# A two-block layer stack on one core: gelu copied out of PSUM in the recurrence, weight splits at phase ends on VectorE, and last products placed behind transposes

## The chip, the core and the metric

The kernel runs on one core of a Trainium2 chip. The metric is the device time of one execution in microseconds. Before the change three runs gave a median of 1570.56 us (1567.63 to 1571.66). One further execution was profiled; everything read from the trace is of that one.

## The reference

The input is one sequence of 256 tokens of width 1024 with a 256-token context. It passes two layers of a first block (latent attention, multi-scale pooling, gated linear attention, merged), then two layers of a second block: an attention layer and a recurrent layer, each followed by a gated feed-forward network. The change touches the second block and the last product of the first. What it computes there, cut to what matters:

```
def rmsnorm_2(x, g):                       # over the 1024 columns
    y = xf * lax.rsqrt(jnp.mean(xf * xf, axis=-1, keepdims=True) + RMS_EPS)
    return y * g

def recurrent_mixer(h, w_in, conv_w, conv_b, w_a, b_a, w_i, b_i, lam, w_out):
    gate, xr = jnp.split(h @ w_in, 2, axis=-1)
    gate = jax.nn.gelu(gate, approximate=True)
    xc = <causal convolution of width 4 on xr, per channel> + conv_b
    r = sigmoid(einsum('bsni,nij->bsnj', xg, w_a) + b_a)     # xg: xc in 4 blocks of 256
    i = sigmoid(einsum('bsni,nij->bsnj', xg, w_i) + b_i)
    log_a = -LRU_C * r * softplus(-lam);  a = exp(log_a)
    u = sqrt(-expm1(2 * log_a)) * (i * xc)
    hs = <scan over tokens: hs[t] = a[t] * hs[t-1] + u[t]>
    return (hs * gate) @ w_out

for layer in range(DEPTH):                 # second block: attention, then recurrence
    x = x + rmsnorm_2(mixer(rmsnorm_2(x, norm_mix_pre)), norm_mix_post)
    x = x + rmsnorm_2(swiglu(rmsnorm_2(x, norm_ffn_pre)), norm_ffn_post)
```

## The kernel before, in words

All matrix products of fp32 data are made of three products of reduced type. An operand is split into a rounded high part and the low rest: for a weight chunk (128 x 1024, 512 KB, tile `wr`) ScalarE copies the high part (`wh`, line 377) and VectorE or GpSimd subtracts it from the raw chunk (`wl`, line 379); for an activation ScalarE does the high part (lines 385, 388) and VectorE the low one (386, 389). A product then takes `high*high`, `low*high` and `high*low` on TensorE (lines 395 to 397), so 24 matmuls for one output tile with eight blocks of 128 in the contraction. There are three buffers for raw chunks and three for split ones, with five more "held" ones at the phase ends, three PSUM tiles `mm` for products and three `at` for transposes, scores and gates.

The engine of a low-part split is chosen by a counter: with `lopool[0] = n` each n-th split goes to GpSimd. `load`, which fetches the weights of a whole phase end, sets n to 6; the recurrence sets it to 3; otherwise it is 0 in the second block, which means VectorE alone.

A scheduler orders the instructions of each engine beforehand, by the order in which the kernel names them, by priorities (`tc.high_priority`) and by its own simulation; on the chip each engine works its queue strictly in that order.

A phase end works like this (`out_proj` for the three mixers, the end of `ffn` for the two feed-forward parts). The tokens stand in two tiles of 128. The output product of tile 0 is made, evicted with a square sum and a gain (`out_evac`, 429 and 579), its norm is taken (GpSimd, 419), it is added to the residual stream `xr` (`residual`, 574), normed for the next phase into `xs` (`prenorm`, 429, 553, 419, 557), transposed on TensorE (560) and split into `xnah` and `xnal` (385, 386). Meanwhile TensorE makes the products of tile 1. In `out_proj` a tile has four products of 24 matmuls; in `ffn` the last chunks of weights are held so that tile 1's share of them can be made after tile 0's.

The recurrence (`recurrent_core`) has these pieces. The gate's first four channel blocks of 128 are made with tokens as rows, passed through gelu and transposed back (`flip`) into `gl`. `conv(i)`, i = 0 to 7, makes a product and applies the four taps, three of them on VectorE straight from PSUM (1414). `gates(n)` makes the two gate products for blocks 2n and 2n+1 (1422) and forms a decay `av`, the inside of the square root `mv` (GpSimd squares `av`, 1434) and `iv`. `states(i0, i1)` takes one square root over four blocks on ScalarE (1441), multiplies on GpSimd (1443) and scans on VectorE (1444). The square root needs another function table in ScalarE than the tanh and exp around it. `gelu(i)` for blocks 4 to 7 makes a product, takes gelu with two multiply-adds that read the product in PSUM (1450, 1452), multiplies with the states (1461) and splits the result into rows of `y` (388, 389), which the output product consumes. In the text the gate blocks 4 to 7 are called halves 4 to 7, after the name the changed code gives them.

Of the kernel before, what the change touches and what calls it, by code (L numbers as in the profile page):

```python
# [9 lines left out]
F32 = mybir.dt.float32  # L10
# [3 lines left out]
OP = mybir.AluOpType  # L14
# [259 lines left out]
def trunk_and_stack(ctx, tc, xin, w, vec, rows, cst, msk, tabs, toep, out):  # L274
# [270 lines left out]
    def prenorm(xn, t, g):  # L545

        xt = xr[:, t, :]
        b = xs_tile(edge)
        ss = sm(2)
        for c in range(2):  # L550
            sq(b[:, c * 512:c * 512 + 512], xt[:, c * 512:c * 512 + 512], ss[:, c:c + 1])
        s1 = sm(1)
        V.tensor_scalar(s1, ss[:, 0:1], ss[:, 1:2], EPS, op0=OP.add, op1=OP.add)
        y = rsqrt(s1, 1)
        for k4 in range(2):
            sl = slice(k4 * 512, k4 * 512 + 512)
            V.scalar_tensor_tensor(b[:, sl], xt[:, sl], y, g[:, sl], op0=OP.mult, op1=OP.mult)
            p = atps()
            for k in range(4):
                T.transpose(p[:, k * P:(k + 1) * P], b[:, (4 * k4 + k) * P:(4 * k4 + k + 1) * P], ident)  # L560
            split(xn, (ALL, slice(4 * k4, 4 * k4 + 4), slice(t * P, t * P + P)), p.rearrange("p (k t) -> p k t", k=4))

# [27 lines left out]
    def load(keys):  # L590

        was = lopool[0]
        lopool[0] = 6
        r = [HW(k) if 2 <= i < 2 + NHOLD else W(k) for i, k in enumerate(keys)]
        lopool[0] = was
        return r

    def out_proj(keyf, a, tiles, ops, after):

        chs = load([keyf(cb, hf) for cb in range(4) for hf in range(2)])  # L600
        for i, (tk, xt, gb) in enumerate(tiles):
            ssp = sm(4)
            for cb in range(4):
                out_evac(as2(chs[2 * cb:2 * cb + 2], a, slice(tk, tk + P)), 256, ops[i], cb * 256, ssp[:, cb:cb + 1], gb)
            with tc.high_priority(offset=600):
                residual(xt, ops[i], ssp, 4)
                after(i)
# [793 lines left out]
    def recurrent_core(xn, y, rp):  # L1401
# [14 lines left out]
        def gates(n):  # L1416
# [8 lines left out]
            for m in range(2):  # L1425
                i = 2 * n + m
                p = gate(ra, m)
                t = rp.tile([P, 256], F32, tag="t", name=nm("rt"), bufs=6)
# [4 lines left out]
                t2 = rp.tile([P, 256], F32, tag="t", name=nm("rt"), bufs=6)  # L1433
# [12 lines left out]
        def gelu2(p):  # L1446

            t = rp.tile([P, 256], F32, tag="t", name=nm("rt"), bufs=6)
# [6 lines left out]
        def gelu(i):  # L1455

            if i < 2 * NR:
                t = gl[:, i, :]
            else:
                t = gelu2(ws(W(("rg", i)), xn, 0, 256))  # L1460
            V.tensor_tensor(t, t, mv[:, i, :], op=OP.mult)
            split(y, (ALL, i), t, 0.25)

        gl = rp.tile([P, 2 * NR, 256], F32, name="gl")
# [9 lines left out]
        for t in range(2):  # L1474
            for i in range(NR):
                late.append((i, t, gelu2(as2(chs[2 * i:2 * i + 2], xn, slice(t * P, t * P + P)))))
# [12 lines left out]
        states(4, 8)  # L1489
        for i in range(8):  # L1490
            gelu(i)
        lopool[0] = 0

    def ffn(l, xn, name):
        with ExitStack() as st:
# [39 lines left out]
            for c in range(2):  # L1535
# [10 lines left out]
                for t in range(2):  # L1546
                    if t == 1:
                        held = held[NHOLD:] + held[:NHOLD]
                        for j, (k2, ch) in enumerate(held):
                            part(pd[1], 1, k2, ch, j == R - 1)  # L1550
                    out_evac(pd[t], 512, ops[t], c * 512, ssp[t][:, c:c + 1], g)
                    if c == 1:
                        with tc.high_priority(offset=600):
                            residual(xr[:, t, :], ops[t], ssp[t], 2)
                            after(t)
# [35 lines left out]
```

## Time and profile before

| what | us |
|---|---|
| median of three runs | 1570.56 |
| the profiled execution | 1570.03 |
| its span in the trace | 1568.3 |
| TensorE busy | 1492.4 |
| VectorE busy | 949.9 |
| ScalarE busy | 756.1 |
| GpSimd busy | 360.9 |

The span runs from the first to the last instruction in the trace; 1.7 us of the profiled execution lie around it. In the trace PE is TensorE, DVE is VectorE, ACT is ScalarE, POOL is GpSimd and SP the engine that issues the transfers. Times in the text such as "at 1334.65" are us from the start of the span. The places in the trace: first block until about 907, its output product until 935, attention 935 to 1043, its output product until 1074, feed-forward until 1263, recurrence 1263 to 1339, its output product until 1365, second feed-forward until the end. A row's `[idle <- releaser]` is how long the engine stood still before the row and what ended that.

### The profile page before, as it was taken

What the parts mean: (1) busy time and instruction counts of PE and PEld (TensorE: products, weight loads), DVE (VectorE), ACT (ScalarE), POOL (GpSimd) and SP (SyncE); (2) the same over time, 40 slices, a digit from 0 to 9 for tenths busy, and PEclk for the clock granted to TensorE, in tenths of its full rate; (3) what the DMA queues carried; (4) which work ended last, traced back from release to release, by engine and by line L of the source; (5) the groups of instructions that cost most, each with busy time, mean ns of one, the idle gap of its engine ahead of it and who ended that gap; (6) DMA issues with size and microseconds to landing.
All of it is one profiled execution on the core that took longest, in us unless ns stands there. A gap on an engine that the chain in (4) does not pass through costs nothing.

```text
span 1568.3 us, 25530 instructions
## 1 busy us (share of the span) xinstructions
PE 1492.4 (95%) x10206; PEld 1284.0 (82%) x10206; DVE 949.9 (61%) x1479; ACT 756.1 (48%) x1267; POOL 360.9 (23%) x276
## 2 busy tenths in 40 slices
PE   6999999999999999998989989989999997899998
PEld 3766668787877789777889989869999887799986
DVE  5555435856445576667694764767665577656654
ACT  4444344453323365755644454554444457534443
POOL 1213125735400002336582020311000034100000
PEclk9999999999999999999999999999999999899999
DMA  8323322222334465224337664425556654435564
GB/s 340 121 103 125 121 90 81 66 76 68 108 110 163 144 189 168 95 74 137 104 133 254 196 217 145 132 85 169 165 186 187 217 187 148 140 130 179 185 187 135
DMA packets 65638, 229.79 MB, mean 147 GB/s; under 512 B 7280, under 2 KB 7920, under 8 KB 65392
## 3 DMA queue, kind: packets, MB, share of 16 engines
q1 hardware_dynamic: 65520, 228.16, 44.9%
q8 instruction: 80, 1.31, 0.3%
q14 instruction: 38, 0.31, 0.1%
HBM read 227.09 MB, written 1.05 MB: 145 GB/s over the span
## 4 chain that ended last, share of the span: by engine, by line
PE 77%; DVE 7%; POOL 4%; issue 4%; DMA 4%; ACT 4%; SPq 0%; POOLq 0%; DVEq 0%; ACTq 0%
PE mm L395 21%; PE mm L397 21%; PE mm L396 21%; DMA wr<-in_w_dram 3%; PE at L735 2%; DVE wl L379 2%; PE aux L768 2%; ACT wh L377 1%; PE at L755 1%; POOL wl L379 1%; POOL E L915 1%; POOL qp L895 1%; PE mm L466 1%; PE at L859 1%; PE aux L466 1%
## 5 line engine op out<-in xcount | busy, mean ns | idle before, releaser
L377 ACT ACTIVATE wh<-wr 128x1024 fp32r<-128x1024 f32 x352 | 370.8, 1055 | 424.9 <-PE mm L396 133.5
L379 DVE TENSOR_TENSOR wl<-wr,wh 128x1024 fp32r<-128x1024 f32 x288 | 363.9, 1265 | 287.2 <-ACT wh L377 285.9
L395 PE MATMUL mm<-xnah,wh 128*128 128x256 f32 (+1 forms) x1192 | 367.9, 309 | 11.2 <-DVE rt L1452 10.3
L397 PE MATMUL mm<-xnah,wl 128*128 128x256 f32 (+1 forms) x1192 | 361.9, 304 | 3.0 <-DVE wl L379 2.1
L396 PE MATMUL mm<-xnal,wh 128*128 128x256 f32 (+1 forms) x1192 | 362.0, 304 | 0.2 <-DVE xnal L386 0.2
L395 PEld LDWEIGHTS mm<-xnah,wh 128*128 128x128 f32 x1192 | 226.6, 190 | 27.8 <-DVE rt L1452 10.6
L379 POOL TENSOR_TENSOR wl<-wr,wh 128x1024 fp32r<-128x1024 f32 (+1 forms) x64 | 158.3, 2473 | 353.3 <-ACT wh L377 268.8
L397 PEld LDWEIGHTS mm<-xnah,wl 128*128 128x128 f32 x1192 | 226.6, 190 | 14.9 <-DVE wl L379 2.7
L396 PEld LDWEIGHTS mm<-xnal,wh 128*128 128x128 f32 x1192 | 226.8, 190 | 10.1 <-issue 1.4
L419 POOL TENSOR_TENSOR sm<-sm,minus_half 128x1 f32<-128x1 f32 (+3 forms) x34 | 25.5, 751 | 628.7 <-DVE sm L567 356.3
L395 PE MATMUL mm<-xnbh,wh 128*128 128x512 f32 (+1 forms) x392 | 138.2, 353 | 0.0
L397 PE MATMUL mm<-xnbh,wl 128*128 128x512 f32 (+1 forms) x392 | 136.9, 350 | 0.0
L396 PE MATMUL mm<-xnbl,wh 128*128 128x512 f32 (+1 forms) x392 | 136.7, 349 | 0.0
L395 PE MATMUL mm<-wh,xnah 128*128 128x256 f32 x288 | 84.3, 294 | 8.5 <-ACT xnah L385 6.3
L395 PEld LDWEIGHTS mm<-xnbh,wh 128*128 128x128 f32 x392 | 75.6, 193 | 11.8 <-issue 2.5
L397 PEld LDWEIGHTS mm<-xnbh,wl 128*128 128x128 f32 x392 | 75.6, 193 | 11.2 <-issue 2.4
L396 PEld LDWEIGHTS mm<-xnbl,wh 128*128 128x128 f32 x392 | 75.7, 193 | 11.0 <-issue 2.1
L396 PE MATMUL mm<-wl,xnah 128*128 128x256 f32 x288 | 83.3, 291 | 1.1 <-POOL wl L379 1.1
L397 PE MATMUL mm<-wh,xnal 128*128 128x256 f32 x288 | 82.6, 290 | 0.7 <-DVE xnal L386 0.7
L396 PE MATMUL mm<-wl,hh 128*128 128x512 f32 x176 | 68.8, 391 | 0.0
L397 PE MATMUL mm<-wh,hl 128*128 128x512 f32 x176 | 68.8, 391 | 0.0
L395 PE MATMUL mm<-yh,wh 128*128 128x512 f32 (+1 forms) x192 | 65.6, 342 | 0.9 <-ACT scr L1030 0.9
(365 smaller groups left out, 2895.5 us busy)
## 6 DMA issues: line engine op xcount, KB each, us to landing
wr<-in_w_dram SPq DMA_DIRECT2D x398, 512.0 KB, 3.6
wr<-in_w_dram SPq DMA_DIRECT2D x18, 256.0 KB, 2.7
row<-in_rows_dram SPq DMA_DIRECT2D x8, 512.0 KB, 5.4
xt<-in_xin_dram SPq DMA_DIRECT2D x4, 512.0 KB, 5.8
scr<-in_rows_dram SPq DMA_DIRECT2D x8, 256.0 KB, 4.8
xr<-in_xin_dram SPq DMA_DIRECT2D x2, 512.0 KB, 4.7
xc<-in_xin_dram SPq DMA_DIRECT2D x2, 512.0 KB, 4.7
toep<-in_toep_dram SPq DMA_DIRECT2D x1, 1024.0 KB, 7.0
```

What stands on the lines that cost most here:

```text
L377: S.activation(ch.h, r, AF.Copy)
L379: eng.tensor_tensor(ch.l, r, ch.h.bitcast(F32), op=OP.subtract)
L395: T.matmul(dst, lh, rh, start=first and i == 0, stop=False)
L396: T.matmul(dst, lh, rl, start=False, stop=False)
L397: T.matmul(dst, ll, rh, start=False, stop=last and i == n - 1)
L419: G.tensor_tensor(y, m, minus_half[:, :n], op=OP.pow)
L466: T.matmul(p[32 * j:32 * j + 32, c0:c0 + 256], sc[:, k * 32:k * 32 + 32], r[:, j, :], start=half == 0, stop=half == 1, tile_position=(0, 3 ...
L735: T.matmul(pa[:, :n], qxs[pr, j][:, c0 + qt * P:c0 + qt * P + P], kxs[pr, j][:, :n], start=True, stop=True)
L755: T.transpose(pa[:, k * 256 + qt * P:k * 256 + qt * P + P], r[qt][:, (2 * k2 + k) * P:(2 * k2 + k + 1) * P], ident)
L768: T.matmul(py[64 * j:64 * j + 64, c0:c0 + 256], v[:, k, h * 64:h * 64 + 64], pTs[j][k // 2][:, k % 2, :], start=k == 0, stop=k == nk - 1, ...
L859: T.matmul(pa[c * s:c * s + s, t * 2 * s:(t + 1) * 2 * s], k_[:, i:i + s], q_[:, :, j:j + s], start=True, stop=True, tile_position=(0, c * s))
L895: (V, G)[j].tensor_tensor(b[r, j, :], gq[r], e[r], op=OP.mult)
```

## The change

- `load` no longer sets `lopool`, and the recurrence no longer sets it to 3: all low-part splits of the second block and of the output product ahead of it go to VectorE. Thirteen GpSimd splits become VectorE splits.
- `gelu2` first copies the product out of PSUM to SBUF (`h`, a ScalarE copy), and the square and both multiply-adds read the copy.
- `gl` holds all eight blocks. The recurrence names its pieces in another order: `conv` 0 to 3, `gates(0)`, `conv` 4 and 5, `gates(1)`, `conv(6)`, the first square root, `conv(7)`, four output blocks, and then the gate halves 4 to 7 between `gates(2)`, `gates(3)` and the second square root. The pool `t` has four buffers in place of six.
- At the phase ends the transposes of tile 0 are returned, and tile 1's last product (in `out_proj` the fourth, 24 matmuls; in `ffn` the last held chunk, six matmuls) is tied behind them on TensorE. At the last phase end there are no transposes and nothing is tied.

```
-        was = lopool[0]
-        lopool[0] = 6
-        r = [HW(k) if 2 <= i < 2 + NHOLD else W(k) for i, k in enumerate(keys)]
-        lopool[0] = was
-        return r
+        return [HW(k) if 2 <= i < 2 + NHOLD else W(k) for i, k in enumerate(keys)]
+
+    def behind(tr):
+        return tc.issue_after(tr.ins) if tr is not None else nullcontext()
...
             for cb in range(4):
-                out_evac(as2(chs[2 * cb:2 * cb + 2], a, slice(tk, tk + P)), 256, ops[i], cb * 256, ssp[:, cb:cb + 1], gb)
+                with behind(tr if cb == 3 else None):
+                    d = as2(chs[2 * cb:2 * cb + 2], a, slice(tk, tk + P))
+                out_evac(d, 256, ops[i], cb * 256, ssp[:, cb:cb + 1], gb)
...
-        def gelu2(p):
-            t = rp.tile([P, 256], F32, tag="t", name=nm("rt"), bufs=6)
-            S.activation(t, p, AF.Square, scale=float(np.sqrt(0.044715)))
-            V.scalar_tensor_tensor(t, t, 1.0, p, op0=OP.add, op1=OP.mult)
+        def gelu2(p, h):
+            S.activation(h, p, AF.Copy)
+            t = rp.tile([P, 256], F32, tag="t", name=nm("rt"), bufs=4)
+            S.activation(t, h, AF.Square, scale=float(np.sqrt(0.044715)))
+            V.scalar_tensor_tensor(t, t, 1.0, h, op0=OP.add, op1=OP.mult)
             S.activation(t, t, AF.Tanh, scale=float(np.sqrt(2 / np.pi)))
-            V.scalar_tensor_tensor(t, t, 1.0, p, op0=OP.add, op1=OP.mult)
-            return t
...
+            V.scalar_tensor_tensor(h, t, 1.0, h, op0=OP.add, op1=OP.mult)
+
+        def out(i):
+            t = gl[:, i, :]
             V.tensor_tensor(t, t, mv[:, i, :], op=OP.mult)
             split(y, (ALL, i), t, 0.25)
...
-        lopool[0] = 3
-        for n in range(4):
-            conv(2 * n)
+        def gate_half(i):
+            gelu2(ws(W(("rg", i)), xn, 0, 256), gl[:, i, :])
+
+        for i in range(4):
+            conv(i)
             if late:
                 flip(*late.pop(0))
-            conv(2 * n + 1)
-            if n:
-                gates(n - 1)
+        gates(0)
+        conv(4)
+        conv(5)
+        gates(1)
+        conv(6)
+        states(0, 4)
+        conv(7)
+        for i in range(4):
+            out(i)
+        gate_half(4)
+        gates(2)
+        gate_half(5)
         gates(3)
-        states(0, 4)
+        gate_half(6)
         states(4, 8)
-        for i in range(8):
-            gelu(i)
-        lopool[0] = 0
+        gate_half(7)
+        for i in range(4, 8):
+            out(i)
...
                         for j, (k2, ch) in enumerate(held):
-                            part(pd[1], 1, k2, ch, j == R - 1)
+                            with behind(tr if c == 1 and j == R - 1 else None):
+                                part(pd[1], 1, k2, ch, j == R - 1)
```

How this moves instructions is seen in the order of each engine. First TensorE at the recurrence's output product, before: `mm_13427` is the fourth and last product of tile 1, `at_13327` and `at_13335` the transposes of tile 0, `mm_13540` the first product of the feed-forward part.

```order
L395 MATMUL mm_13427<-wh_13194,xnbh_12358 128x256
L396 MATMUL mm_13427<-wl_13195,xnbh_12358 128x256
L397 MATMUL mm_13427<-wh_13194,xnbl_12359 128x256
L560 MATMUL at_13327<-ct,xs_13318 128x128 x4
L560 MATMUL at_13335<-ct,xs_13318 128x128 x4
L395 MATMUL mm_13540<-wh_13494,xnah_13144 128x256
```

And the same place now, where `mm_13411` is the third product of tile 1, `mm_13439` the fourth (24 matmuls, three shown) and `mm_13552` the first of the feed-forward part.

```order
L395 MATMUL mm_13411<-wh_13194,xnbh_12358 128x256
L396 MATMUL mm_13411<-wl_13195,xnbh_12358 128x256
L397 MATMUL mm_13411<-wh_13194,xnbl_12359 128x256
L560 MATMUL at_13339<-ct,xs_13330 128x128 x4
L560 MATMUL at_13347<-ct,xs_13330 128x128 x4
L395 MATMUL mm_13439<-wh_13200,xnbh_12358 128x256
L396 MATMUL mm_13439<-wl_13201,xnbh_12358 128x256
L397 MATMUL mm_13439<-wh_13200,xnbl_12359 128x256
```

The transposes have moved ahead of the fourth product. The output products of the first block are reordered in the same way, the end of the first feed-forward part by six matmuls; at attention's output product the transposes stood ahead of the fourth product already, and TensorE's order is unchanged there.

ScalarE at the recurrence's output product, before: `wh_13494` to `wh_13524` are the first six weight chunks of the feed-forward part, `scr` the evictions of tile 1's products, `xnah` the high part of tile 0's transposes.

```order
L429 ACTIVATE scr_13396,sm_13342<-mm_13371 128x256
L377 ACTIVATE wh_13512<-wr_13510 128x1024
L429 ACTIVATE scr_13424,sm_13342<-mm_13399 128x256
L377 ACTIVATE wh_13518<-wr_13516 128x1024
L377 ACTIVATE wh_13524<-wr_13522 128x1024
L429 ACTIVATE scr_13452,sm_13342<-mm_13427 128x256
L385 ACTIVATE xnah_13144<-at_13327 128x4x128
```

And now (the six chunks are `wh_13506` to `wh_13536`):

```order
L429 ACTIVATE scr_13408,sm_13354<-mm_13383 128x256
L377 ACTIVATE wh_13524<-wr_13522 128x1024
L429 ACTIVATE scr_13436,sm_13354<-mm_13411 128x256
L377 ACTIVATE wh_13530<-wr_13528 128x1024
L385 ACTIVATE xnah_13156<-at_13339 128x4x128
L385 ACTIVATE xnah_13156<-at_13347 128x4x128
L377 ACTIVATE wh_13536<-wr_13534 128x1024
L429 ACTIVATE scr_13464,sm_13354<-mm_13439 128x256
```

The high part of the transposes stands behind the fifth chunk in place of the sixth.

VectorE in the middle of the recurrence, before, around the last taps of `conv(7)` (`mm_12851`): the scans are `mv<-av,iv`, the output blocks `gl<-gl,mv`.

```order
L1414 SCALAR_TENSOR_TENSOR xconv<-mm_12851,vt,xconv 128x253
L1444 SCALAR_TENSOR_TENSOR mv_12366<-av,iv 128x256
L1430 TENSOR_SCALAR rt_12887<-rt_12887,nsp 128x256
L1444 SCALAR_TENSOR_TENSOR mv_12366<-av,iv 128x256
L1438 SCALAR_TENSOR_TENSOR iv<-iv,xconv 128x256
L1414 SCALAR_TENSOR_TENSOR xconv<-mm_12851,vt,xconv 128x254
L1444 SCALAR_TENSOR_TENSOR mv_12366<-av,iv 128x256
L1461 TENSOR_TENSOR gl<-gl,mv_12366 128x256
L1444 SCALAR_TENSOR_TENSOR mv_12366<-av,iv 128x256
L1461 TENSOR_TENSOR gl<-gl,mv_12366 128x256
L1414 SCALAR_TENSOR_TENSOR xconv<-mm_12851,vt,xconv 128x255
```

And now (`conv(7)` is `mm_12868`, `wl_13104` the split for half 7, `gl` also holds the copies of the halves):

```order
L1448 SCALAR_TENSOR_TENSOR mv_12366<-av,iv 128x256 x2
L1462 TENSOR_TENSOR gl<-gl,mv_12366 128x256
L379 TENSOR_TENSOR wl_13104<-wr_13101,wh_13103 128x1024
L1418 SCALAR_TENSOR_TENSOR xconv<-mm_12868,vt,xconv 128x254
L389 SCALAR_TENSOR_TENSOR xnbl_12359<-gl,xnbh_12358 128x256
L1455 SCALAR_TENSOR_TENSOR rt_12941<-rt_12941,gl 128x256
L1434 TENSOR_SCALAR rt_12953<-rt_12953,nsp 128x256
L1442 SCALAR_TENSOR_TENSOR iv<-iv,xconv 128x256
L1418 SCALAR_TENSOR_TENSOR xconv<-mm_12868,vt,xconv 128x255
```

Here repeated rows between them are left out. The last tap of `conv(7)` now stands behind all four scans and output blocks, two of their low parts and the split for half 7. Further down, six of the eight low-part splits for the output product stand ahead of the last `mv` of `gates(3)`, where it was three on VectorE before.

## Rows read from the trace of the kernel before

**Rows 1.** The page, busy time and share of each engine.
```profile
PE 1492.4 (95%) x10206; PEld 1284.0 (82%) x10206; DVE 949.9 (61%) x1479; ACT 756.1 (48%) x1267; POOL 360.9 (23%) x276
```

**Rows 2.** PE's timeline: start us, us, operation, count, idle before and its releaser.
```profile
915.35 0.38 PE L396 MATMUL mm<-wl,moh 128*128 128x256 f32 x1 [1.81 <-POOL wl L379]
933.63 0.39 PE L395 MATMUL mm<-wh,xnah 128*128 128x256 f32 x1 [1.12 <-ACT xnah L385]
...
1048.19 0.38 PE L396 MATMUL mm<-wl,xnbh 128*128 128x256 f32 x1 [1.28 <-DVE wl L379]
...
1071.18 0.38 PE L395 MATMUL mm<-wh,xnbh 128*128 128x256 f32 x1 [0.88 <-DVE op L579]
1263.49 0.39 PE L395 MATMUL mm<-wh,xnah 128*128 128x256 f32 x1 [0.82 <-ACT xnah L385]
1264.89 0.38 PE L397 MATMUL mm<-wh,xnal 128*128 128x256 f32 x1 [0.65 <-DVE xnal L386]
...
1334.65 0.58 PE L395 MATMUL mm<-xnah,wh 128*128 128x256 f32 x1 [10.35 <-DVE rt L1452]
...
1369.78 0.58 PE L395 MATMUL mm<-wh,xnah 128*128 128x256 f32 x1 [3.79 <-ACT xnah L385]
```

**Rows 3.** Stretches: length, busy (x count) by engine, granted PE clock, DMA, GB/s.
```profile
935.00:940.00 5.00, 4.91 (x28) 4.70 (x28) 4.58 (x7) 2.59 (x6) 2.70 (x2) 0.66 0.76 275
...
1320.00:1350.00 30.00, 18.23 (x129) 17.30 (x128) 20.49 (x39) 18.60 (x34) 8.94 (x8) 0.83 0.52 158
1335.00:1340.00 5.00, 5.00 (x30) 5.00 (x30) 4.88 (x8) 2.60 (x5) 0.27 (x1) 0.65 0.51 137
...
1370.00:1375.00 5.00, 5.00 (x24) 4.95 (x25) 5.00 (x7) 2.83 (x5) 2.99 (x2) 0.50 0.64 212
...
1380.00:1385.00 5.00, 5.00 (x45) 5.00 (x44) 1.62 (x3) 1.36 (x3) 0.00 (x0) 1.00 0.13 51
```

**Rows 4.** GpSimd's timeline, at splits and in the recurrence.
```profile
912.95 2.35 POOL L379 TENSOR_TENSOR wl<-wr,wh 128x1024 fp32r<-128x1024 f32 x1 [66.69 <-DMA wr<-in_w_dram]
...
1254.71 2.90 POOL L379 TENSOR_TENSOR wl<-wr,wh 128x1024 fp32r<-128x1024 f32 x1 [0.15 <-ACT wh L377]
...
1291.48 2.37 POOL L379 TENSOR_TENSOR wl<-wr,wh 128x1024 fp32r<-128x1024 f32 x1 [6.57 <-ACT wh L377]
...
1318.95 3.16 POOL L1434 TENSOR_TENSOR rt<-av 128x256 f32<-128x256 f32 x1 [3.57 <-ACT av L1431]
```

**Rows 5.** VectorE's operations of 1255 to 1350 by form: count, busy us, mean ns.
```profile
L379 DVE TENSOR_TENSOR wl<-wr,wh 128x1024 fp32r<-128x1024 f32 x17 | 21.0, 1241 | 8.5 <-ACT wh L377 8.5
L1444 DVE TENSOR_TENSOR_SCAN mv<-av,iv 128x256 f32<-128x256 f32 x8 | 5.5, 698 | 0.0
...
L1461 DVE TENSOR_TENSOR rt<-rt,mv 128x256 f32<-128x256 f32 x4 | 1.6, 405 | 0.0
```

**Rows 6.** VectorE's timeline.
```profile
1045.47 2.67 DVE L379 TENSOR_TENSOR wl<-wr,wh 128x1024 fp32r<-128x1024 f32 x1 [0.67 <-ACT wh L377]
...
1254.60 3.57 DVE L574 SCALAR_TENSOR_TENSOR xr<-op,sm,xr 128x512 f32<-128x512 f32 x2
...
1266.29 1.42 DVE L574 SCALAR_TENSOR_TENSOR xr<-op,sm,xr 128x512 f32<-128x512 f32 x2 [0.86 <-POOL sm L419]
...
1291.89 1.00 DVE L1414 SCALAR_TENSOR_TENSOR xconv<-mm,vt,xconv 128x253 f32<-128x253 f32 x2 [0.64 <-ACT xconv L1411]
...
1305.82 0.41 DVE L1435 SCALAR_TENSOR_TENSOR mv<-rt,rt 128x256 f32<-128x256 f32 x1
...
1317.09 0.47 DVE L1414 SCALAR_TENSOR_TENSOR xconv<-mm,vt,xconv 128x255 f32<-128x255 f32 x1
```

**Rows 7.** ScalarE's timeline.
```profile
1331.36 1.06 ACT L1441 ACTIVATE mv<-mv 128x1024 f32<-128x1024 f32 x1
...
1340.26 0.42 ACT L388 ACTIVATE xnbh<-rt 128x256 fp32r<-128x256 f32 x1 [2.66 <-DVE rt L1461]
...
1353.64 0.38 ACT L429 ACTIVATE scr<-mm 128x256 f32<-128x256 f32 x1 [3.03 <-PE mm L397]
...
1367.83 1.06 ACT L377 ACTIVATE wh<-wr 128x1024 fp32r<-128x1024 f32 x1 [3.00 <-DMA wr<-in_w_dram]
```

**Rows 8.** The page, transfers by form: count, KB each, median us to landing.
```profile
wr<-in_w_dram SPq DMA_DIRECT2D x398, 512.0 KB, 3.6
```

More of the change, by code (lines that the diff above doesn't have):

```diff
@@ L1 @@
-from contextlib import ExitStack
+from contextlib import ExitStack, nullcontext
 import numpy as np
@@ L1432, in gates @@
                 S.activation(t, t, AF.Tanh, scale=-1.0)
-                t2 = rp.tile([P, 256], F32, tag="t", name=nm("rt"), bufs=6)
+                t2 = rp.tile([P, 256], F32, tag="t", name=nm("rt"), bufs=4)
                 G.tensor_tensor(t2, av[:, i, :], av[:, i, :], op=OP.mult)
@@ L1444, in states @@
                 V.tensor_tensor_scan(mv[:, i, :], av[:, i, :], iv[:, i, :], 0.0, op0=OP.mult, op1=OP.add)
-        def gelu2(p):
-            t = rp.tile([P, 256], F32, tag="t", name=nm("rt"), bufs=6)
-            S.activation(t, p, AF.Square, scale=float(np.sqrt(0.044715)))
-            V.scalar_tensor_tensor(t, t, 1.0, p, op0=OP.add, op1=OP.mult)
-            S.activation(t, t, AF.Tanh, scale=float(np.sqrt(2 / np.pi)))
-            V.scalar_tensor_tensor(t, t, 1.0, p, op0=OP.add, op1=OP.mult)
-            return t
[L1455 to L1460, printed above, removed]
+        def gelu2(p, h):
+            S.activation(h, p, AF.Copy)
+            t = rp.tile([P, 256], F32, tag="t", name=nm("rt"), bufs=4)
+            S.activation(t, h, AF.Square, scale=float(np.sqrt(0.044715)))
+            V.scalar_tensor_tensor(t, t, 1.0, h, op0=OP.add, op1=OP.mult)
+            S.activation(t, t, AF.Tanh, scale=float(np.sqrt(2 / np.pi)))
+            V.scalar_tensor_tensor(h, t, 1.0, h, op0=OP.add, op1=OP.mult)
+        def out(i):
+            t = gl[:, i, :]
             V.tensor_tensor(t, t, mv[:, i, :], op=OP.mult)
             split(y, (ALL, i), t, 0.25)
-        gl = rp.tile([P, 2 * NR, 256], F32, name="gl")
+        gl = rp.tile([P, 8, 256], F32, name="gl")
         chs = load([("rgt", i, hf) for i in range(NR) for hf in range(2)])
@@ L1475, in recurrent_core @@
             for i in range(NR):
[L1476 removed]
+                h = rp.tile([P, 256], F32, tag="t", name=nm("rt"), bufs=4)
+                gelu2(as2(chs[2 * i:2 * i + 2], xn, slice(t * P, t * P + P)), h)
+                late.append((i, t, h))
                 if len(late) > 1:
                     flip(*late.pop(0))
[L1479 to L1481 removed]
+        def gate_half(i):
+            gelu2(ws(W(("rg", i)), xn, 0, 256), gl[:, i, :])
+        for i in range(4):
+            conv(i)
             if late:
                 flip(*late.pop(0))
[L1484 to L1486 removed]
+        gates(0)
[10 more added lines that the diff above has]
+        gate_half(5)
         gates(3)
[L1488 removed]
+        gate_half(6)
         states(4, 8)
[L1490 to L1492 removed]
+        gate_half(7)
+        for i in range(4, 8):
+            out(i)
     def ffn(l, xn, name):
@@ L1554, in ffn @@
                             residual(xr[:, t, :], ops[t], ssp[t], 2)
-                            after(t)
+                            tr = after(t)
         return nxt
```

6 lines of the change are left out of this document (4 added, 2 removed).

## Prediction

> **What bounds the kernel now.** I read the page's engines first: TensorE is busy 1492.4 us of 1568.3 [rows 1], so it bounds the kernel. A faster operation on another engine is worth nothing except where TensorE waits for it. Next came TensorE's timeline, for its waits at the places that the change touches: eight rows, of which the one at 1334.65 (10.35 us) and the one at 1369.78 (3.79 us) are over 2 us [rows 2]. Third, the stretches behind those waits. A 5 us stretch at full speed holds 45 matmuls; behind the 3.79 us wait one holds 24 at a granted clock of 0.50, which is the 1.2 GHz level of the two (1.2 and 2.4), and behind the 10.35 us wait 30 at 0.65 [rows 3]. So a long wait costs twice: once as idle time, once as slow matmuls. Last came the timelines of the engines that end these waits: GpSimd's splits [rows 4], VectorE by form and by time [rows 5, 6], ScalarE [rows 7] and the transfers [rows 8]. I sum against the profiled execution, 1570.0 us, 0.5 below the median of the runs.
>
> **GpSimd's splits go to VectorE.** A split takes 2.35 to 2.90 us on GpSimd [rows 4] and 1.24 on VectorE [rows 5]. At 915.35 TensorE waited 1.81 us for a GpSimd split; on VectorE it is ready 2.35 - 1.24 = 1.1 us sooner: **-1.1**. At 1048.19 it waited 1.28 us for a VectorE split that took 2.67 us [rows 6], more than twice the normal, while GpSimd split another chunk. Without that neighbour it takes 1.24, 1.4 less, but VectorE now does both, and I count **-1.1** (bounds 0 and -1.3).
>
> The other side of this edit is VectorE's load: 13 x 1.24 = 16 us more. Outside the recurrence VectorE is idle 39% of the span [rows 1], and the splits fall where it waits for ScalarE's high part (8.5 us of idle time in front of 17 splits [rows 5]). Where it is not covered it shows in the recurrence, below.
>
> The residual additions show the same contention: two of them took 3.57 us beside a GpSimd split that ran from 1254.71, and 1.42 us later, beside none [rows 4, 6]. The Trainium skill, page "SBUF — State Buffer", section "Who interferes with whom", has it that a VectorE instruction with two SBUF inputs contends with a GpSimd instruction that reads SBUF, and one with at most one SBUF input does not. Our trace agrees: two taps that take the product from PSUM ran 1.00 us, undelayed, beside a split from 1291.48 [rows 4, 6]. The rule speaks against one edit, since gelu's multiply-adds now read two SBUF operands. If half of the eight were stretched by the residual pair's factor, 3.57 / 1.42 = 2.5, that would be 4 x 0.41 x 1.5 = 2.5 us, and the sum by this rule 12.8 in place of the 15.3 below. I do not count it.
>
> **Phase ends.** (a) First block's output product. Now 24 matmuls (24 x 0.11 = 2.7 us, from 45 in 5 us) stand between tile 0's transposes and the next phase. They cover the 1.12 us wait for `xnah` and most of the slow stretch 935 to 940, which has 28 matmuls in place of 45, so (45 - 28) x 0.11 = 1.9 us. Against that, TensorE reaches the transposes 2.7 us sooner and meets `xs` before it is ready: I put a new wait of 1.3 us there, and 0.3 for less cover later. **-1.4** (bounds 0, -3.0).
> (b) Attention. TensorE's order is unchanged. The 0.88 us wait for an eviction goes, since VectorE's residual is no longer stretched: **-0.9** (bounds 0, -1.2).
> (c) First feed-forward part. The waits are 0.82 + 0.65 = 1.5 us [rows 2]. Six matmuls now lie behind the transposes (0.7 us), and the residual pair is 3.57 - 1.42 = 2.1 us shorter: **-1.3** (bounds 0, -1.5).
> (d) Recurrence's output product. The fourth product of tile 0 is evicted at 1353.64 [rows 7], and the feed-forward part starts 16.1 us later at 1369.78, at half clock. ScalarE stands 3.00 us there for a chunk [rows 7], and the transposes' high part is queued behind that chunk, the sixth. In the new order it is behind the fifth. By counts TensorE passes three products (72 x 0.11 = 8 us), the transposes (about 1), then the fourth (2.7): some 12 us after the eviction, when `xnah` and `xnal` are about ready. The idle time of 3.79 goes, and with it the slow clock: (45 - 24) x 0.11 = 2.3 in 1370 to 1375 and about 0.4 beyond. **-6.5** (bounds -3.8, if the clock still falls, and -6.9). This is the surest and largest term. If the sixth chunk were still ahead, the 3.00 would remain.
>
> **Recurrence.** The 10.35 us wait at 1334.65 is one for a gelu multiply-add (line 1452) that frees a PSUM tile; it is late because tanh stood behind the second square root (1331.36) and its table load. The copy frees that tile at once, so this wait in this form goes. In all 129 matmuls stand in 1320 to 1350, where 270 would fit: 141 x 0.11 = 15.7 us are lost there [rows 3]. The question is what is late next, and I think it is VectorE. Its queue from 1306.2 (end of the `mv` at 1305.82 [rows 6]) to the last tap of `conv(7)` now holds three splits (3 x 1.24), six taps (6 x 0.47), four scans (4 x 0.70), four output blocks (4 x 0.40), and two low parts and three small operations (5 x 0.40; no row, taken as line 1461's): 3.7 + 2.8 + 2.8 + 1.6 + 2.0 = 12.9 us, and an estimated 1 us in which it waits for the first square root. So the tap ends at 1320.1; before it ended at 1317.6, and GpSimd's square of the next `av` followed at 1318.95 [rows 4], which shows `gates(3)` right behind that tap. TensorE waits 2.5 us here.
> From there the last `mv` comes 2.5 us later or more, since six splits stand ahead of it on VectorE where three stood (3.7 us more, most of it in idle time). The second square root's end goes from 1332.4 to about 1336.3: 2.5 from the tap, and 1.4 because the weight copies ahead of it on ScalarE wait for chunks that land 3.6 us after their issue [rows 8]. The first row of `y` (1340.26 before, 7.8 after the square root) now comes 4.6 after it, because two splits (2.5 us) and two multiply-adds (0.8) which stood between are done earlier: 1340.9. TensorE, free of gelu, is through with everything else near 1332, and stands some 9 us. Resuming at half clock costs it 1.2 as I guess from the 15 matmuls missing in 1335 to 1340 (15 x 0.11 = 1.7). New loss 2.5 + 9.0 + 1.2 = 12.7 against 15.7: **-3.0**. The bounds are far apart. At best only the tap's 2.5 and a short wait of some 3 remain: -10. At worst the square root stands behind two more landings (2 x 3.6): +4.2. I take -3.0, since the chain to the square root is read from rows and moves by little.
> The eight copies out of PSUM (8 x 0.4 = 3 us, as an eviction in [rows 7]) lie in ScalarE's idle time, half of its span [rows 1]; without that cover they'd delay the square root by under 2. That the halves of the square root are apart changes nothing: the number of table loads is the same. Four buffers of `t` in place of six suffice for four gate halves. Cost 0.
>
> **Sum:** 1.1 + 1.1 + 1.4 + 0.9 + 1.3 + 6.5 + 3.0 = 15.3; 1570.0 - 15.3 = 1554.7, so 1555.
>
> **Rivals.**
> 1. The recurrence gives nothing or gives back up to 3 us: the `y` rows are as late as ever because the square root is, and VectorE's splits delay it further. For it: VectorE's queue there is nearly full (20.49 of 30 us in 1320 to 1350 [rows 3]). Against: the rows of `y` have less ahead of them. Time: 1570.0 - 12.3 to -9.3, so 1558 to 1561.
> 2. The recurrence's stall goes almost wholly: the `y` rows of blocks 0 to 3 carry TensorE until the others come. For it: by the walk above these four are ready by 1320. Against: only the part of the output product that reads them can run, and the PSUM tiles are few. Time: the best bound, 1570.0 - 12.3 - 10 = 1548, or 1545 with (a) and (b) at their best.
> 3. Slower: VectorE's queue becomes the bound in the phases. All 13 splits, 16 us, come to lie on the path: at the transposes `xs` waits behind the splits of the coming phase, and TensorE, parked in order behind the transposes, cannot go on with the fourth product that it used to do first. Decisive is whether VectorE's idle time between a phase end's evictions is under 1.24 us a split. For it: in (a) and (d) the transposes are moved before products that were cover. Against: VectorE's 8.5 us of waiting in 17 splits, and the shorter residual. With the gains down to 6.5 of (d): 1570.0 + 16 - 6.5 = 1580.
> 4. No change: the new order waits at each transposes for `xs` as long as it waited before for `xnah` (gains of (a), (c), (d) idle gone, 7), and the recurrence gives back 4: about 1567 to 1572.
>
> **How the numbers follow.** A difference of 0.3% (4.7 us) is about what a measurement of this kernel can tell from none. My forecast (terms within 1549 to 1561, recurrence from -9 to +1) has 0.52; rival 1 0.18, with a little beyond 1561; rival 2 0.10; rival 3 0.08; rival 4 0.12. Faster: 0.52 + 0.18 + 0.10 = 0.80; same 0.12; slower 0.08. For the range, 1546 to 1567 holds the forecast, rival 1, most of 2 and a little of 4, some 0.83. The likeliest case's own range is 1549 to 1561.
>
> **What would show it.** Right: no GpSimd split behind 907; the wait near 915 under 0.7 us; residual pairs of 1.4 us at every phase end; at the recurrence's output product no wait for `xnah`, and a clock of 1.00 after it (d), with the feed-forward part some 12 us behind the eviction of tile 0's fourth product in place of 16.1; in the recurrence a wait of some 2.5 us for a tap of `conv(7)`, then one of about 9 us for a high part of `y` in place of line 1452. Wrong: a wait of over 3 us at any transposes for `xs` (rival 3 or 4); the second square root behind 1340 and a recurrence wait over 13 us; or no wait over 4 us there at all (rival 2).

## The result and the profile after

The changed kernel took 1556.31 us (median of 6 runs, 1554.82 to 1562.77) against 1570.4 before: ratio 0.9922, 95% interval 0.9905 to 0.9939. A second comparison, below, gave 0.994 (0.9922 to 0.9959). The forecast was 1555.

TensorE stays the bound; GpSimd has lost thirteen splits, 32.9 us of its busy time. The page of the kernel after, engines:

```profile
PE 1484.8 (96%) x10206; PEld 1275.4 (82%) x10206; DVE 954.2 (61%) x1492; ACT 758.1 (49%) x1275; POOL 328.0 (21%) x263
```

TensorE's timeline after, at the places of [rows 2]:

```profile
912.85 0.38 PE L396 MATMUL mm<-wl,moh 128*128 128x256 f32 x1 [0.64 <-DVE wl L379]
927.74 1.32 PE L560 MATMUL at<-ct,xs 128*128 128x128 f32 x8 [1.57 <-DVE xs L557]
...
1047.40 0.39 PE L396 MATMUL mm<-wl,xnbh 128*128 128x256 f32 x1 [0.88 <-DVE wl L379]
1063.09 1.32 PE L560 MATMUL at<-ct,xs 128*128 128x128 f32 x8 [1.33 <-DVE xs L557]
...
1257.57 0.39 PE L397 MATMUL mm<-wh,xnal 128*128 128x256 f32 x1 [0.58 <-DVE xnal L386]
1309.15 1.13 PE L1426 MATMUL at<-xconv,wr 128*128 128x256 f32 x4 [0.61 <-ACT rt L1433]
1324.05 0.38 PE L395 MATMUL mm<-wh,xnbh 128*128 128x256 f32 x1 [1.05 <-ACT gl L1452]
1336.10 0.58 PE L395 MATMUL mm<-wh,xnbh 128*128 128x256 f32 x1 [9.85 <-ACT xnbh L388]
...
1362.01 0.38 PE L397 MATMUL mm<-wh,xnal 128*128 128x256 f32 x1 [0.64 <-DVE xnal L386]
```

The GpSimd wait of 1.81 is a VectorE wait of 0.64. The waits for `xnah` of 1.12 and 3.79 are gone. The wait for `xs` of 1.57 at the first block's transposes is new; the one of 1.33 at attention's is not, it was 1.20 before:

```profile
1068.98 1.31 PE L560 MATMUL at<-ct,xs 128*128 128x128 f32 x8 [1.20 <-DVE xs L557]
```

The 10.35 us wait for line 1452 has become one of 9.85 for the high part of the first late row of `y`.

Stretches after (columns as in [rows 3]): behind the 9.85 us wait, and behind the recurrence's output product, where before 24 matmuls stood at 0.50:

```profile
1335.00:1340.00 5.00, 3.25 (x13) 2.96 (x14) 5.00 (x13) 1.59 (x4) 0.00 (x0) 0.50 0.38 110
1340.00:1345.00 5.00, 4.70 (x25) 4.50 (x23) 0.25 (x3) 0.73 (x5) 0.00 (x0) 0.60 0.00 0
...
1362.00:1367.00 5.00, 4.99 (x41) 4.99 (x42) 5.00 (x8) 3.07 (x7) 0.55 (x1) 1.00 0.82 243
```

At attention's end, too, a residual pair took 3.57 us before, beside a GpSimd split from 1063.21:

```profile
1062.68 3.57 DVE L574 SCALAR_TENSOR_TENSOR xr<-op,sm,xr 128x512 f32<-128x512 f32 x2 [0.33 <-POOL sm L419]
```

VectorE after: the residual pairs at that place and at the one of [rows 6], the last tap of `conv(7)`, the last `mv`, and two multiply-adds of gelu with a scan behind the first:

```profile
1056.66 1.42 DVE L575 SCALAR_TENSOR_TENSOR xr<-op,sm,xr 128x512 f32<-128x512 f32 x2 [0.34 <-POOL sm L419]
1248.46 1.41 DVE L575 SCALAR_TENSOR_TENSOR xr<-op,sm,xr 128x512 f32<-128x512 f32 x2
1312.74 0.47 DVE L1418 SCALAR_TENSOR_TENSOR xconv<-mm,vt,xconv 128x255 f32<-128x255 f32 x1
1327.51 0.42 DVE L1439 SCALAR_TENSOR_TENSOR mv<-rt,rt 128x256 f32<-128x256 f32 x1
1332.33 0.68 DVE L1457 SCALAR_TENSOR_TENSOR gl<-rt,gl 128x256 f32<-128x256 f32 x1 [2.59 <-ACT rt L1456]
1332.94 1.21 DVE L1448 TENSOR_TENSOR_SCAN mv<-av,iv 128x256 f32<-128x256 f32 x1
1336.12 0.39 DVE L1457 SCALAR_TENSOR_TENSOR gl<-rt,gl 128x256 f32<-128x256 f32 x1
```

ScalarE after: two weight copies that waited for their chunks, the second square root, the first late row of `y`, the eviction of tile 0's fourth product, and the high part of the transposes ([rows 7]):

```profile
1322.31 1.06 ACT L377 ACTIVATE wh<-wr 128x1024 fp32r<-128x1024 f32 x1 [0.64 <-DMA wr<-in_w_dram]
1325.28 1.06 ACT L377 ACTIVATE wh<-wr 128x1024 fp32r<-128x1024 f32 x1 [0.97 <-DMA wr<-in_w_dram]
1329.51 1.06 ACT L1445 ACTIVATE mv<-mv 128x1024 f32<-128x1024 f32 x1
1335.63 0.42 ACT L388 ACTIVATE xnbh<-gl 128x256 fp32r<-128x256 f32 x1 [2.08 <-DVE gl L1462]
1348.48 0.38 ACT L429 ACTIVATE scr<-mm 128x256 f32<-128x256 f32 x1 [3.01 <-PE mm L397]
1360.00 1.07 ACT L385 ACTIVATE xnah<-at 128x512 fp32r<-128x512 f32 x2
```

Events that both traces have cut the spans into stages. "Recurrence" runs from its first matmul with `xnal` to the eviction of tile 0's fourth product; "its end" from there to the first transposes inside the second feed-forward part (`flip`). Times in us, one profiled execution each:

```
stage                            before  after  again  ties   splits ties+  recur-
                                                              alone  splits rence
up to first block's out product  904.2   902.0  902.3  905.1  901.0  904.6  901.3
that product and attention       125.1   123.9  124.3  126.7  126.3  124.1  125.7
attention's product, ffn 1a      172.0   168.8  168.4  170.6  171.8  169.3  173.3
ffn 1b and its end                63.6    62.9   62.4   65.0   63.0   62.6   63.9
recurrence                        88.8    90.9   90.8   90.0   90.8   91.7   91.3
its end                           31.4    25.5   24.8   25.5   26.4   24.6   28.5
rest                             183.2   180.3  180.2  184.0  180.5  181.4  183.3
```

Of the 14.0 us between the first two columns, 8.9 lie in the five stages of my sum: 1.2, 3.2, 0.7, -2.1 and 5.9. The other 5.1 lie ahead of the change's first place (2.2) and in the last feed-forward part (2.9).

A single trace is not the kernel's median: the traced execution of the ties alone took 1568.64 us and that of the splits alone 1561.52, where their medians below are 1563.09 and 1566.42. Kernels that share the code of a stage are further traces of it. The stages of the phase ends, by what the phase ends have (us, in fourteen traces):

```
stage                            neither (3)    ties (2)     splits (2)   both (7)
that product and attention       125.1 to 125.7 126.5, 126.7 126.3, 128.9 123.1 to 127.6
attention's product, ffn 1a      172.0 to 173.3 170.5, 170.6 171.8, 172.3 168.4 to 170.7
ffn 1b and its end               63.6 to 63.9   62.9, 65.0   63.0, 63.2   62.3 to 63.0
the recurrence's end             28.5 to 31.4   25.5, 25.5   26.4, 26.5   24.6 to 25.7
```

The 127.6 is the trace of the late copies below; the other six of its row end at 124.3.

### The profile page after: what moved, and what is told of

Same layout as the page of the kernel before. It is cut to its first block, busy times and chain, and to the rows that moved or that the text cites. A ratio compares the mean times of both kernels' runs of the same rounds, so it can differ in the third digit from the quotient of the medians.

```text
span 1554.3 us, 25545 instructions
## 1 busy us (share of the span) xinstructions
PE 1484.8 (96%) x10206; PEld 1275.4 (82%) x10206; DVE 954.2 (61%) x1492; ACT 758.1 (49%) x1275; POOL 328.0 (21%) x263
## 3 DMA queue, kind: packets, MB, share of 16 engines
HBM read 227.09 MB, written 1.05 MB: 147 GB/s over the span
## 4 chain that ended last, share of the span: by engine, by line
PE 77%; DVE 7%; DMA 6%; ACT 4%; POOL 3%; issue 3%; SPq 0%; POOLq 0%; DVEq 0%; ACTq 0%
PE mm L395 21%; PE mm L397 21%; PE mm L396 21%; DMA wr<-in_w_dram 5%; DVE wl L379 3%; PE at L739 2%; PE aux L772 2%; ACT wh L377 2%; PE at L759 1%; POOL E L919 1%; POOL qp L899 1%; PE mm L466 1%; PE aux L466 1%; POOL wl L379 1%; PE at L863 1%
## 5 line engine op out<-in xcount | busy, mean ns | idle before, releaser
L379 DVE TENSOR_TENSOR wl<-wr,wh 128x1024 fp32r<-128x1024 f32 x301 | 378.9, 1261 | 280.5 <-ACT wh L377 278.6
L397 PEld LDWEIGHTS mm<-xnah,wl 128*128 128x128 f32 x1192 | 224.9, 189 | 15.7 <-DVE wl L379 3.2
L379 POOL TENSOR_TENSOR wl<-wr,wh 128x1024 fp32r<-128x1024 f32 (+1 forms) x51 | 126.5, 2481 | 247.6 <-ACT wh L377 229.7
L395 PE MATMUL mm<-wh,xnbh 128*128 128x256 f32 x192 | 56.4, 297 | 13.7 <-ACT xnbh L388 9.8
```

The lines of the kernel that those rows point to most:

```text
L379: eng.tensor_tensor(ch.l, r, ch.h.bitcast(F32), op=OP.subtract)
L395: T.matmul(dst, lh, rh, start=first and i == 0, stop=False)
L397: T.matmul(dst, ll, rh, start=False, stop=last and i == n - 1)
```

## The experiments

Each ratio is against the kernel before on the same chip. The traces read with the same columns.

**Ties alone.** Only the phase ends are changed:

```
+                with behind(tr if cb == 3 else None):
+                    d = as2(chs[2 * cb:2 * cb + 2], a, slice(tk, tk + P))
```

> The kernel before with tile 1's last products tied behind tile 0's transposes at the phase ends, and nothing else of the change. Theory A (order carries the largest part): the recurrence's output product gains 6 (the feed-forward part starts some 12 us behind the eviction of tile 0's fourth product in place of 16.1), the other phase ends 1 to 2 together; 1562 to 1564. Theory B (GpSimd's splits carry it, the order only shows once they are gone): within 2 us of before, 1568 to 1572.

1563.09 against 1569.16, ratio 0.9966 (0.9951 to 0.9981). Theory A. The recurrence's end gains 5.9, but the first block's product costs 1.6, since the transposes wait longer for `xs` than after. VectorE makes it beside a GpSimd split there, in 2.93 us for 1.42 after:

```profile
930.31 2.93 DVE L557 SCALAR_TENSOR_TENSOR xs<-xr,sm,row 128x512 f32<-128x512 f32 x2
932.63 1.50 PE L560 MATMUL at<-ct,xs 128*128 128x128 f32 x8 [2.17 <-DVE xs L557]
```

**Splits alone.**

```
-        lopool[0] = 6
...
-        lopool[0] = 3
```

> The kernel before with all 13 low-part splits on VectorE and nothing else of the change. Theory A: 3 to 4 us are gained at the loads and phase ends of the first block, attention and the first feed-forward part, and 2 to 3 are given back in the recurrence, where VectorE's queue is late; 1567 to 1570. Theory B (contention with GpSimd is what held the phases): 8 to 10 us faster, 1560 to 1562, with the wait before the feed-forward part gone as well.

1566.42, ratio 0.9986 (0.9971 to 1.0001): theory A on the time, but not on the places. The first block's product and attention lose 1.2 where it had a gain, and 5.0 come from the recurrence's end; the recurrence gives back 2.0 as it said. Nothing holds the order at the phase ends here: the scheduler puts the transposes behind the fourth product again, at attention's end too, where before they stood ahead of it, and TensorE waits for `xnah` at both. In the recurrence the wait for line 1452 (here 1448) grows from 10.35 to 13.32:

```profile
933.35 0.39 PE L395 MATMUL mm<-wh,xnah 128*128 128x256 f32 x1 [2.15 <-ACT xnah L385]
...
1069.88 0.38 PE L395 MATMUL mm<-wh,xnah 128*128 128x256 f32 x1 [1.68 <-ACT xnah L385]
...
1335.98 0.58 PE L395 MATMUL mm<-xnah,wh 128*128 128x256 f32 x1 [13.32 <-DVE rt L1448]
```

**Copy alone.** gelu reads the copy, the pieces stand in the order of before:

```
+            S.activation(h, p, AF.Copy)
...
         for i in range(8):
             gelu(i)
```

> The kernel before with gelu copied out of PSUM (eight-block gl, four buffers of t), pieces in the order of before, splits and phase ends as before. Theory A: the 10.35 us wait for line 1452 turns into one of 8 to 10 us for the first high part of y, since the second square root and what follows it on VectorE set that time; 1567 to 1573. Theory B (the held PSUM tile was the bound): the wait falls under 4 us, 1560 to 1563.

1569.8, ratio 1.0006 (0.9991 to 1.002): theory A on the time. The single wait became four of together 10.6 us:

```profile
1333.42 0.58 PE L395 MATMUL mm<-wh,xnbh 128*128 128x256 f32 x1 [5.80 <-ACT wh L377]
1334.74 0.58 PE L396 MATMUL mm<-wl,xnbh 128*128 128x256 f32 x1 [0.74 <-DVE wl L379]
1339.64 0.58 PE L395 MATMUL mm<-wh,xnbh 128*128 128x256 f32 x1 [2.18 <-ACT xnbh L388]
1343.16 0.58 PE L397 MATMUL mm<-wh,xnbl 128*128 128x256 f32 x1 [1.87 <-DVE xnbl L389]
```

So the held PSUM tile was where TensorE stood, not what bounded it.

**Recurrence alone.** The copy and the new order of pieces, a third of its splits still on GpSimd:

```
+        states(0, 4)
+        conv(7)
...
+        gate_half(4)
+        gates(2)
```

> The kernel before with the changed recurrence (copy and new order of pieces), its splits still one in three on GpSimd, phase ends as before. Theory A: the new order puts scans, output blocks and gate halves ahead of what the second square root needs; the wait is 9 to 11 us and a wait for the tap of conv(7) is added; 1569 to 1574. Theory B (the step of the prediction): the rows of y come 3 us earlier against their product; 1566 to 1568.

1569.67, ratio 1.001 (0.9994 to 1.0026): theory A. The second square root starts 20.4 us after the last tap of `conv(7)` (1316.74 to 1337.11); it was 14.3 before and 14.6 with the copy alone. The wait for the first late row is 8.52; the wait for the tap that theory A added is not there.

```profile
1337.11 1.06 ACT L1441 ACTIVATE mv<-mv 128x1024 f32<-128x1024 f32 x1
```

```profile
1343.04 0.58 PE L395 MATMUL mm<-wh,xnbh 128*128 128x256 f32 x1 [8.52 <-ACT xnbh L388]
```

**The changed kernel again.** No edit.

> The changed kernel once more, for a narrower ratio and a second trace. If the 2.5 us that the first pair of traces differed before 877 us, in work that the change leaves alone, and the closer spacing of matmuls in the last feed-forward part (1000 of them in 117.6 us against 119.7) belong to one execution, they are gone here and the ratio comes nearer to 0.994; if they belong to the kernel, they stay and the ratio is 0.991 to 0.993.

1559.36 against 1569.9, ratio 0.994 (0.9922 to 0.9959). The lead ahead of the first block's product stays at 1.9 us, but other kernels with the same code there begin that product anywhere from 901.0 to 907.5, so it can't be credited to the change. The second half is mixed: the closer spacing stays in this trace, yet the ratio moved toward 0.994.

**Ties and splits, old recurrence.**

```
-        lopool[0] = 3
         for n in range(4):
             conv(2 * n)
```

> The changed phase ends and splits with the recurrence of before. Theory A (the new recurrence gives nothing of its own; order and splits at the phase ends help each other): 1557 to 1560, within 2 us of the changed kernel. Theory B (the new recurrence repairs what the splits on VectorE cost there, seen as a 13.3 us wait in the kernel with the splits alone): 1561 to 1563, some 4 us slower than the changed kernel.

1559.46, ratio 0.9942 (0.9919 to 0.9964), the same as the changed kernel: theory A. Its wait in the recurrence is longer, at little cost, since the rows of `y` come about as late in both: the high part of the first late row starts 76.9 us into the stage here and 78.1 in the changed kernel, and the stage ends after 91.7 and 90.9. TensorE's waits there:

```profile
1316.34 1.56 PE L1426 MATMUL at<-xconv,wr 128*128 128x256 f32 x6 [1.27 <-DVE xconv L1418]
1335.18 0.58 PE L395 MATMUL mm<-xnah,wh 128*128 128x256 f32 x1 [13.61 <-DVE rt L1456]
```

**Ties and recurrence, GpSimd's splits kept.**

```
+        lopool[0] = 6
...
+        lopool[0] = 3
```

> The changed phase ends and recurrence with one split in six or three still on GpSimd. Theory A: the ties alone gave 6 and the recurrence 0, so 1563; what the changed kernel has beyond that needs the splits on VectorE. Theory B (GpSimd's splits do no harm once the order is changed): 1557 to 1560.

1568.05, ratio 0.9984 (0.9967 to 1.0001). Worse than either theory. What makes it slower than the ties alone stays open: its trace (1567.88 us) has the recurrence 1.1 us longer (91.2 for 90.0), but the traced execution of the ties alone was as long as this one (1568.64), so the two traces do not hold the difference of the medians.

**Splits and recurrence, no ties.**

```
-                with behind(tr if cb == 3 else None):
```

> The changed kernel without the ties at the phase ends. Theory A (ties and splits help each other at the phase ends, the recurrence gives nothing): some 8 us of the changed kernel's gain go, 1566 to 1568, as the kernel with the splits alone. Theory B (the new recurrence and splits carry it): 1560 to 1562.

1566.15, ratio 0.9967 (0.9953 to 0.9982). Theory A: without the ties most of the gain goes. The first block's product and attention take 128.9 us here against 123.9; the splits alone had 126.3 with the same code there.

**Gates first.** The order of pieces that I thought better:

```
+        gates(2)
+        gates(3)
         for i in range(4):
             out(i)
         gate_half(4)
-        gates(2)
```

> The changed kernel with gates(2) and gates(3) named ahead of output blocks 0 to 3 and of gate halves 4 to 6. Theory A (gate halves and output blocks ahead of what the second square root needs make it late: it starts 16.3 us after the last tap of conv(7) in the changed kernel, 13.8 before): it starts 14 us or less after it, the wait for the first high part of y falls from 9.85 to some 7, and the time by 2 to 3 us. Theory B (landings of weight chunks ahead of it on ScalarE set it, whatever the order): within 1 us of the changed kernel.

1559.31, ratio 0.9945 (0.9928 to 0.9962): theory B on the time. The square root still starts 16.7 us behind the tap (1318.05 to 1334.71), so naming the gates first gained nothing by itself. Weight copies ahead of it waited for their chunks for 2.91, 0.85 and 0.57 us. The wait for the first late row did fall, to 7.76, but waits of 2.67 ahead of it and 2.98 for a low row took its place:

```profile
1323.35 1.06 ACT L377 ACTIVATE wh<-wr 128x1024 fp32r<-128x1024 f32 x1 [2.91 <-DMA wr<-in_w_dram]
1334.71 1.06 ACT L1445 ACTIVATE mv<-mv 128x1024 f32<-128x1024 f32 x1
```

**Late copies.** The last three chunks of the output product behind the square root:

```
+            with behind(root[0] if k[0] == "ro" and i >= 5 else None):
+                r.append(HW(k) if 2 <= i < 2 + NHOLD else W(k))
```

> The changed kernel with the high-part copies of the output product's last three chunks tied behind the second square root on ScalarE. Theory A (chunks that land late hold ScalarE's queue ahead of the second square root): it starts 14 to 15 us after the last tap of conv(7) in place of 16.8, the wait falls by 2 us and so does the time. Theory B (the chain through gates(3) sets it): 16 us or more, the time within 1 us of the changed kernel, or later since the copies come late.

1559.0, ratio 0.9921 (0.99 to 0.9941), not to be told from the changed kernel. Theory A on the start of the square root: it comes 14.4 us behind the tap (1317.87 to 1332.31), and the wait falls to 7.29. That landings held it is not shown apart: five weight copies of 1.06 us stand between tap and square root here, seven in the changed kernel, and the waits for chunks there fell from 1.61 to 0.35. The late splits on VectorE then hold a low row, and the recurrence as a whole gains 1.2 us (89.7 for 90.9):

```profile
1338.38 0.58 PE L395 MATMUL mm<-wh,xnbh 128*128 128x256 f32 x1 [7.29 <-ACT xnbh L388]
1342.95 0.58 PE L397 MATMUL mm<-wh,xnbl 128*128 128x256 f32 x1 [2.93 <-DVE xnbl L389]
```

**Unread matmuls in the wait.** 72 products of data at hand, into a PSUM tile that nobody reads:

```
+            if i == 3:
+                with tc.issue_after(x.ins):
+                    p = atps()[:, :256]
+                    for j in range(NWARM):
+                        x = T.matmul(p, lh, rh, start=j == 0, stop=j == NWARM - 1)
```

> The changed kernel with 72 matmuls whose result nobody reads, in TensorE's queue of the recurrence's output product between the part that needs blocks 0 to 3 of y and the part that needs blocks 4 to 7; they fill some 8 us of the 9.85 us wait. Theory A (the wait costs twice: 38 matmuls run at half clock in the 8 us behind it): those run at full clock, and the eviction of tile 0's fourth product comes 3 to 4 us sooner after the second square root than the 19.0 of the changed kernel; 3 us faster than it. Theory B (the rows of y come one by one and TensorE waits for them, so its speed there is hidden): within 1 us of the changed kernel.

1555.96, ratio 0.9903 (0.9876 to 0.9929); the interval overlaps those of the changed kernel, so the whole time alone does not prove the gain. The trace shows it in this stretch: 64 of the 72 run in the wait (the other eight behind it, at 1342.14), the clock stays at 1.00, and the eviction comes 15.7 us behind the square root, where both traces of the changed kernel have 19.0. Theory A, 3.3 us. TensorE's, the stretch's and ScalarE's rows:

```profile
1331.39 7.84 PE L613 MATMUL at<-wh,xnbh 128*128 128x256 f32 x64
1341.56 0.39 PE L395 MATMUL mm<-wh,xnbh 128*128 128x256 f32 x1 [2.33 <-ACT xnbh L388]
```

```profile
1340.00:1345.00 5.00, 3.06 (x23) 2.86 (x24) 5.00 (x12) 1.59 (x4) 0.00 (x0) 1.00 0.32 107
```

```profile
1334.91 1.06 ACT L1465 ACTIVATE mv<-mv 128x1024 f32<-128x1024 f32 x1
1350.62 0.38 ACT L429 ACTIVATE scr<-mm 128x256 f32<-128x256 f32 x1 [2.40 <-PE mm L397]
```

**Both of these**, with fewer unread matmuls for the shorter wait.

```
+    NWARM = 64
```

> The changed kernel with both of the last edits: the output product's last three high-part copies behind the second square root, and 64 unread matmuls in the wait for y. Theory A (the two costs are separate: the square root comes 2.3 us sooner with the first, half clock goes with the second): from the last tap of conv(7) to the eviction of tile 0's fourth product some 31 us (35.7 in the changed kernel, 32.3 and 34.4 with one edit each), the ratio to before 0.987 to 0.990. Theory B (with the late copies VectorE's splits hold the low rows of y, a 2.93 us wait there, and that wait brings the low clock back or takes the gain): 32 us or more, no better than the unread matmuls alone, 0.990.

1556.65, ratio 0.9917 (0.9899 to 0.9935): theory B. From the tap to the eviction it takes 34.5 us (1316.47 to 1351.00), no better than the late copies alone. Behind a wait of 2.64 us for a low row the clock is low again, 0.77 in the stretch:

```profile
1341.64 0.39 PE L397 MATMUL mm<-wh,xnbl 128*128 128x256 f32 x1 [2.64 <-DVE xnbl L389]
```

```profile
1340.00:1345.00 5.00, 3.35 (x19) 3.36 (x20) 3.26 (x8) 1.17 (x3) 0.00 (x0) 0.77 0.56 184
```

## Why the prediction was right, and where it was wrong

The time came out at 1556.31 for 1555, but not by my sum; that the number is so near is in part luck. The signs came: no GpSimd split behind 907, 0.64 us at the load, residual pairs of 1.4 us, no wait for `xnah` at the recurrence's output product, one of 9.85 for a high part of `y`. One did not, the 2.5 us wait for a tap. By the terms, before less after:

- Load and phase end of the first block: 2.5 forecast, 1.2 measured (with attention). The load wait fell by 1.2 as said. The phase end did not pay. The new wait for `xs` (1.57; 1.3 forecast) took most of what the `xnah` wait and the slow clock gave back. It pays only with both edits: ties alone cost 1.4 and 1.6 there, splits alone 1.2 and 3.8, and with both six of seven traces gain 0.8 to 2.0; the seventh, of the late copies, loses 2.5, and I have no cause for it.
- Attention's output product: 2.0 forecast, 3.2 measured. The wait for VectorE's split at the load fell only from 1.28 to 0.88, and the wait of 0.88 for an eviction went as I said, with the residual pair down from 3.57 to 1.42. What I had not counted is a wait for a weight copy on ScalarE that fell from 1.95 at 1054.57 to 1.05 at 1050.03.
- First feed-forward part: 1.3 forecast, 0.7 measured; a wait of 0.58 for `xnal` is left.
- Recurrence's output product: 6.5 forecast, 5.9 measured. The feed-forward part starts 12.2 us behind the eviction (1348.48 to 1360.66) for 16.1, as forecast; the fifth chunk in place of the sixth and the full clock behind it are in the order and the rows. The ties alone give the same 5.9. But splits alone give 5.0 and the copy alone 2.9 (28.6 us for this stage) without the tie, so part of what [rows 7] show there is how a chunk's landing happened to fall.
- Recurrence: 3.0 gained forecast, 2.1 lost measured. This step failed, in the chain to the first late row of `y` and in the price of the slow clock behind it. The tap ends where I said: the stage begins 7.3 us earlier than before (1257.57 for 1264.89), so its end at 1313.2 is 1320.5 in the time of before; I had 1320.1. But TensorE does not wait for it. The wait for `y` is there (9.85 for 9.0). Of the 5.1 us between forecast and measurement, 2.0 lie ahead of the first late row: it starts at 1342.9 in the time of before (1335.63 + 7.3) for 1340.9. The second square root ends 1.6 us later than I had (1330.57 + 7.3 = 1337.9 for 1336.3). Between tap and square root ScalarE makes seven weight copies where it made five, and works on the gate halves; its waits for chunks there, 0.64 and 0.97, are about the 1.4 that I had counted. That leaves the work ahead of the square root as what I had too small; no run shows it apart. The other 3.1 lie behind that row: from it to the eviction it takes 12.9 us (1335.63 to 1348.48), where the forecast left 9.7. "Resuming at half clock costs it 1.2" was wrong: 13 and 25 matmuls stand in the two stretches from 1335 to 1345, the slow clock lasted some 8 us, and the unread matmuls put its price at 3.3; with them the 12.9 become 9.5 (1341.09 to 1350.62).

The terms that I summed to 15.3 thus measured 8.9. The ratio of the second comparison, 0.994 of 1569.9, is 9.4 (6.4 to 12.2), near that; the first pair's 12 to 14 holds the run's own lead ahead of the change and the 2.9 us of the last feed-forward part, of which I had foreseen nothing. By the measured terms alone the time would be 1561.1, the upper end of rival 1's range. Rival 1 (the recurrence gives something back) is the mechanism that the runs support, within the 4.2 us that I gave as the worst bound: the kernel with ties and splits and the old recurrence takes the same time as the changed one.

The contention of [rows 4, 6] carries over to the new operands: a multiply-add of gelu took 0.68 us at 1332.33, while GpSimd worked at its four multiplications from 1330.64, and 0.39 at 1336.12, after them (GpSimd's row, after):

```profile
1330.64 2.95 POOL L1447 TENSOR_TENSOR iv<-iv,mv 128x256 f32<-128x256 f32 x4 [5.55 <-ACT mv L1445]
```

The page "SBUF — State Buffer" of the Trainium skill, section "Who interferes with whom", has this rule for two SBUF inputs, and this trace agrees. Its price was some 0.3 us for that multiply-add, not the 2.5 that I had worked out for four. The scan behind it paid too: 1.21 us at 1332.94, where the next one, at 1335.52, took 0.68. Both stand ahead of the first late row.

## What to carry to other kernels

Ask of a wait not only what ends it but what would end the next one: the copy out of PSUM freed TensorE at once and gave nothing, since the rows it needed came as late as before. Try two edits of one path together before dropping either: at the first block's end each alone cost time and both together gained. Over the whole kernel they came out as 6 for the ties, 3 for the splits and 10 for both with the old recurrence, and as 2, 4 and 10 with the new one; with some 3 us of uncertainty on each, that they help each other beyond adding up is not shown there. A long idle time of TensorE is also paid behind it, here with 3.3 us for 9.85, and where nothing real could fill it, unread matmuls kept the clock.

## What the hardware showed unexpectedly

```profile
1410.00:1460.00 50.00, 50.00 (x419) 50.00 (x418) 30.80 (x43) 23.30 (x36) 0.00 (x0) 1.00 0.56 185
```

```profile
1400.00:1450.00 50.00, 50.00 (x429) 50.00 (x428) 31.17 (x46) 24.28 (x36) 0.00 (x0) 1.00 0.61 185
```

The first row is of before, the second of after: the same kind of matmuls in the last feed-forward part, TensorE never idle, the granted clock 1.00 in both, and yet 419 against 429 in 50 us. From the last `flip` to the first matmul with `hh` the traces took 98.14 us or 95.97, with nothing between: 98.14 in before, the ties alone, the copy alone and the recurrence alone, 95.97 in the other ten. It is 2.2 us of the measured difference. The same stretch in the first feed-forward part took 97.05 us in eleven traces, before and after among them, and 98.14 in the splits alone, the recurrence alone, and splits and recurrence without ties: three levels 1.1 us apart, and a kernel can have one in the first layer and another in the second. What sets it stays open; in the last part it goes neither with the ties alone nor with GpSimd's splits, since ties and recurrence together, with those splits kept, show 95.97.
